# A decoder layer on one core: zero-padded score queries, cached memory in fours, the last FFN features padded, one group for the states' products

## The chip, the cores and the metric

The kernel runs on one core of a Trainium2 chip. The metric is the device time of one execution in microseconds (us); the median of three runs of the kernel before is 990.26 us (988.76 to 992.15).

## What is computed

One layer of a hybrid decoder, for 512 prompt rows and for 8 sampled sequences of 4 rows (32 sample rows) with the same weights, in 32-bit floats. Cut to what matters here:

```python
h = rms_norm(x, g_mix_pre); z = h @ w_in
# mLSTM heads (4 x 128): C is the state, one 128x128 matrix per sequence and head
num = w_inter * einsum('bhtd,bhde->bhte', qc, C) + ...      # product of queries and old state
C_new = decay * C + einsum('bhsd,bhse->bhde', wk, vc)
# differential attention (4 heads, two 64-dim components c, v = 128)
s = einsum('bqhcd,bkhcd->bhcqk', q, k) * DA_QK_DIM ** -0.5
p = softmax(where(mask, s, -inf)); a = p[:, :, 0] - lam * p[:, :, 1]
# prompt: 4 causal blocks of 128 queries; sample: 256 cached keys from pages
x = x + rms_norm(concat(h_ml, h_da) @ w_out, g_mix_post)
# cross attention (4 heads x 256) to 256 memory tokens; for the sample rows
# keys and values are cached: cache_mem_k, cache_mem_v (8, 256, 4, 256)
x = x + rms_norm(mem_attend(rms_norm(x, g_mem_pre), mk, mv) @ w_mo, g_mem_post)
# ConvFFN with 2752 = 21 * 128 + 64 features
u = h @ w_up; c = causal_conv3(u); f = (silu(g) * a) @ w_down
x = x + rms_norm(f, g_ffn_post)
```

## The kernel before

The program is one long list of work that a scheduler orders for each engine from the dependences, the buffers of the pools and its own estimates; the code's order is where it starts from. TensorE (PE) multiplies, VectorE (DVE) and ScalarE (ACT) evacuate and do the softmax arithmetic, GpSimd (POOL) helps, and SyncE's queue (SP) issues nearly all loads.

Weights go through `W`: a 512 KB load into a stage tile `wst` (pool `stg`, six of 128x1024), then `split` writes it as two f32r parts (ACT casts the high part, DVE subtracts for the low part) into a slot of pool `wp` (tag W, four slots `wslot`). A product is three f32r matmuls (L386 to L388 in `gemmA`, L1645 to L1647 for the FFN's second product). An f32 matmul that is not split takes two passes, so it shows as two rows in the trace.

A matmul can use part of the 128x128 array. The profile shows the tile as rows*columns behind the operation: `64*128` contracts over 64 rows, `128*32` gives 32 output partitions, as the sample's products do (32 rows for each of four heads, in four column tiles side by side).

The places that the change touches, in the order of time:

- `mls_update` (L954 to L959): for each head and each half of the eight sequences, the product of the queries `qzm` with the old states `csts` (`mlsi`), the new key-value product `mlus` (L957), and four state updates on VectorE (L959). The 32 `mlsi` products are made in two parts: 16 at the first step of the first half of the sequences, 16 at the first step of the second.
- `da_soft` (L1180, L1181): scores of one query block and head for the two components. Component 0 lies in partitions 0 to 63 of `dqT` and `dkT`, component 1 in 64 to 127; each score matmul takes its 64 rows, then a bf16 matmul adds the causal mask `cb`. Softmax follows on VectorE and ScalarE, the transposes `tpa` (L1196) and the product `oda` with the values (L1206). Block b has (b+1) * 128 keys, 16 block-head pairs in all. Between them the sample's cached keys are transposed (`tpk`, L1159) and scored (`ssc`, L1165), and the cached values are multiplied (`ops`, L1248).
- Cross attention: `mk_load`, `mk_turn` (16 half-sequences of cached keys, eight transposes `tpk` each, L1385) and `mk_scores` (8 matmuls `ssc` per sequence, L1395), one sequence after another with two turns between; `mv_load` (L1400) brings 1 MB of values per sequence into a W slot `vt`; `mv_out` (L1405) makes 8 matmuls `pso` per sequence. The prompt's own steps (scores `sca` L1336, transposes `cpt` L1354, values `cpo` L1366) are interleaved. The eight loads of `w_mo` share the stage tiles with the keys and the W slots with the values.
- FFN: 22 groups of features; the last one has 64 rows. `slotA` loads and splits the 64 rows of `w_down` by themselves, and the last products of L1645 to L1647 (and the sample's, L366) contract over 64 rows.

Of the kernel before, what the change touches and what calls it, by code (L numbers as in the profile page):

```python
# [7 lines left out]
F32 = mybir.dt.float32  # L8
# [7 lines left out]
P = 128  # L16
DM = 1024
SEQ = 512
NB = 8
# [54 lines left out]
def kernel(ctx: ExitStack, tc: tile.TileContext, I, O):  # L74
# [146 lines left out]
    def slotA(w, k0, n0, nrow=256, share=False):  # L221
        def emit():
            st, s = v2(stage(), 512), slot_tile()
            sv = s.rearrange("p l (k n) -> p l k n", k=2)
            r0 = k0 * P
            if nrow == 256:
                dma(out=st, in_=w[r0:r0 + 256, n0:n0 + 512].rearrange("(k p) n -> p k n", p=P))
                split_w(sv, st, share)
            else:
                for k, n in ((0, P), (1, nrow - P)):  # L230
                    dma(out=st[:n, k, :], in_=w[r0 + k * P:r0 + k * P + n, n0:n0 + 512])
                    split(sv[:n, 0, k, :], sv[:n, 1, k, :], st[:n, k, :])
            return sv, st
        W.add(emit)

# [712 lines left out]
    def mls_update(i):  # L948
        g, h = i // H, i % H
        cs_t = csts[g, h]  # L950
        if h == 0:
            for b in range(4):
                for k in range(H):
                    mm(pi[NS * k:NS * k + NS, 0:P], lhsT=qzm[:, 256 * k + (4 * g + b) * NS:256 * k + (4 * g + b + 1) * NS],  # L954
                       rhs=csts[g, k][:, b, :], start=(g + b == 0), stop=(g == 1 and b == 3))
        pu = at("mlus")
        mm(pu, lhsT=kS[:, h, :], rhs=vzs[i], start=True, stop=True)  # L957
        for b in range(4):
            STT(out=cs_t[:, b, :], in0=cs_t[:, b, :], scalar=dec[:, h, 4 + 4 * g + b:5 + 4 * g + b], in1=pu[:, b * P:(b + 1) * P],  # L959
                op0=MUL, op1=ADD)  # L960
        dma(out=O["s_ml_C"][0, 4 * g:4 * g + 4, h].rearrange("b d e -> d b e"), in_=cs_t)
        F.run(2.5)
# [207 lines left out]
    def da_soft(i):  # L1170
        b, h = i // H, i % H
        c0 = b * P
        nk = c0 + P
        pt = pts[i] = N("pda").rearrange("p (c k) -> p c k", c=2)
        nm = small(2, "nm")
        su = small(2, "su")
        sv = [mmp("sda")[:, :nk] for _ in range(2)]
        for c in range(2):
            rr = slice(64 * c, 64 * c + 64)
            mm(sv[c], lhsT=dqT[rr, h, c0:c0 + P], rhs=dkT[rr, h, 0:nk], start=True, stop=False)  # L1180
            mm(sv[c][:, c0:nk], lhsT=identb, rhs=cmaskb, start=False, stop=True)  # L1181
# [4 lines left out]
        nc.vector.reciprocal(out=rc, in_=su)  # L1186
# [191 lines left out]
    def mk_turn(i):  # L1378
        b, c = i // 2, i % 2
        if c == 0:  # L1380
            kts[b] = wp.tile([P, 8, 256], F32, name="kT", tag="W")
        for q in range(2):
            ps = at("tpk")
            for j in range(4):
                tr(ps[:, j * P:(j + 1) * P], kst[i][:, (4 * q + j) * P:(4 * q + j + 1) * P], ident)  # L1385
            (VCP if q else nc.scalar.copy)(out=kts[b][:, 4 * q:4 * q + 4, c * P:(c + 1) * P], in_=v2(ps, P))

    def mk_scores(i):
        b, c = i // 2, i % 2
        if c == 0:  # L1390
            return
        ps = mmp("ssc")[:, :256]
        for c in range(2):
            for h in range(H):
                mm(ps[NS * h:NS * h + NS], lhsT=qs[:, 2 * h + c], rhs=kts[b][:, 2 * h + c, :], start=(c == 0), stop=(c == 1))  # L1395
        sample_exp(sall, b, ps, nm, su)

    def mv_load(b):
        vts[b] = wp.tile([P, 2, DM], F32, name="vt", tag="W")
        dma(out=vts[b], in_=I["cache_mem_v"][0, b].rearrange("(c p) h d -> p c (h d)", p=P))  # L1400

    def mv_out(b):
        for c in range(2):
            for h in range(H):
                mm(pso[NS * h:NS * h + NS], lhsT=az[c][:, h, b * NS:(b + 1) * NS], rhs=vts[b][:, c, 256 * h:256 * h + 256],  # L1405
                   start=(b == 0 and c == 0), stop=(b == NB - 1 and c == 1))

    sall = S([P, NB, 256], F32, "cas")
    nm, su = small(NB, "snm"), small(NB, "ssu")
# [4 lines left out]
    for i, _ in enumerate(gemmB(hqT, [ev_q(m) for m in range(4, 8)])):  # L1414
        if i % 4 == 3:
            for j in (i // 2 - 1, i // 2):
                mk_turn(j)
                mk_load(j + 6)
    for b in range(NB):
        mk_scores(2 * b + 1)  # L1420
        if b < 4:
            for j in (2 * b + 8, 2 * b + 9):
                mk_turn(j)
                if j + 6 < 2 * NB:
                    mk_load(j + 6)
        else:
            mv_load(b - 4)
        if b % 2 == 1:
            next(prompt, None)
# [4 lines left out]
    for n0 in (0, 512):  # L1434
        slotsA(w_mo, n0)
    W.nslots = NSLOT
    for b in range(NB):
        if b >= 4:
            mv_load(b)
    W.pump()  # L1440
    for b in range(NB):
        mv_out(b)
        if b in VSTEPS:
            next(prompt, None)
    run(prompt)
    oS = Z("oS")[:, :256]
    nc.scalar.copy(out=oS, in_=pso)
# [106 lines left out]
    def gate(j, ua, ug, act, i):  # L1554
# [9 lines left out]
        VTT(out=a[:, :SEQ], in0=ca[:n, :SEQ], in1=cg[:n, :SEQ], op=MUL)  # L1564

        def sv(c):
            return c[:n, SEQ:].rearrange("p (b j) -> p b j", j=6)[:, :, 2:6]
        VTT(out=v2(a[:, SEQ:], TS), in0=sv(ca), in1=sv(cg), op=MUL)
        split(act[i // 2][:n, i % 2, 0, :], act[i // 2][:n, i % 2, 1, :], a)
        t = sm.tile([P, NS], F32, name="acs", tag="acs", bufs=5)  # L1570
        nc.gpsimd.tensor_copy(out=t[:n], in_=a[:, SEQ:])
        return t[:n]

    gf = gbc("g_ffn_post")
    acts, acss = {}, {}
# [44 lines left out]
    for gi, js in enumerate(groups):  # L1620
# [8 lines left out]
        behind = []  # L1629

        def one(b, ps, i, s):
            n = P if js[i] < 21 else 64
            t = act[i // 2][:n, i % 2]
            st, en = i == 0, i == nk - 1
            if b == 4:

# [5 lines left out]
                return  # L1642
            s = s[0]
            c0 = b * P
            mm(ps, lhsT=t[:, 0, c0:c0 + P], rhs=s[:n, 0, i % 2, :], start=st, stop=False)  # L1645
            mm(ps, lhsT=t[:, 0, c0:c0 + P], rhs=s[:n, 1, i % 2, :], start=False, stop=False)  # L1646
            mm(ps, lhsT=t[:, 1, c0:c0 + P], rhs=s[:n, 0, i % 2, :], start=False, stop=en)  # L1647

        def add_y(b, ps, n0):
            c = slice(n0, n0 + 512)  # L1650
# [152 lines left out]
```

## Time and profile before

| | before |
|---|---|
| median of 3 runs | 990.26 us |
| range | 988.76 to 992.15 us |
| profiled execution, its own time | 989.55 us |
| span in the profile | 987.8 us |
| mean granted TensorE clock | 0.993 |

How to read the rows: a group shows line, engine, operation, output<-inputs, shape and count, then busy time and the mean of one in ns, then idle time before it and what released it. A timeline row shows start, busy time, line and count; rows overlap because matmuls are pipelined, so the distance of two starts is the price of what lies between. An idle gap before a row is in square brackets with its releaser. The PE row of the page, in 40 slices, is at 9 tenths or more nearly everywhere:

```profile
PE   8999999999999999999999999999999999999994
DVE  6835325645786257633653569827757675685677
ACT  5754313334576357633543433342312222222232
POOL 6610000115231214400000354201100010110114
```

### The profile page before, as it was taken

How to read it: one execution, taken by the hardware profiler on the slowest of the kernel's cores; microseconds unless marked ns; L12 is line 12 of the kernel's file. 1: busy time of each engine (PE TensorE's matmuls, PEld its weight loads, DVE VectorE, ACT ScalarE, POOL GpSimd, SP SyncE). 2: the span in 40 equal slices, each digit the busy share in tenths (PEclk: the TensorE clock that was granted, in tenths of full speed). 3: DMA queues.
4: the chain of work that ended last, by engine and by line, in shares of the span. 5: the costliest groups of instructions: out<-in, count | busy, mean ns of one | idle time of the engine just before them, and what ended most of it. 6: DMA issues, size and time to landing. Idle time of an engine off the chain costs nothing.

```text
span 987.8 us, 17060 instructions
## 1 busy us (share of the span) xinstructions
PE 962.1 (97%) x6615; PEld 811.1 (82%) x6615; DVE 603.4 (61%) x1129; ACT 389.1 (39%) x746; POOL 195.5 (20%) x389
## 2 busy tenths in 40 slices
PE   8999999999999999999999999999999999999994
PEld 5899777789655878898767889989987997997983
DVE  6835325645786257633653569827757675685677
ACT  5754313334576357633543433342312222222232
POOL 6610000115231214400000354201100010110114
PEclk9999999999899999999999999999999999999998
DMA  8950222260835068765841764063053214304113
GB/s 283 301 161 1 86 75 91 63 206 12 255 109 177 21 219 266 261 219 168 304 171 49 233 197 127 6 171 86 4 139 103 74 42 117 118 26 141 31 47 112
DMA packets 120401, 130.26 MB, mean 132 GB/s; under 512 B 8423, under 2 KB 85832, under 8 KB 120320
## 3 DMA queue, kind: packets, MB, share of 16 engines
q1 hardware_dynamic: 114136, 125.69, 41.1%
q10 hardware_dynamic: 6184, 3.48, 1.2%
q8 instruction: 52, 0.85, 0.3%
q14 instruction: 29, 0.24, 0.1%
HBM read 112.22 MB, written 16.93 MB: 131 GB/s over the span
## 4 chain that ended last, share of the span: by engine, by line
PE 83%; DMA 6%; DVE 5%; issue 2%; ACT 2%; POOL 1%; SPq 1%; DVEq 0%; POOLq 0%; ACTq 0%
PE mm L455 30%; PE mm L386 5%; PE mm L387 5%; PE mm L388 5%; PE mm L443 5%; PE mm L1645 4%; PE mm L1647 4%; PE mm L1646 4%; PE mm L366 3%; PE sda L1180 2%; DMA xb<-x_d 2%; PE tpk L1385 2%; DMA xb<-in_x_prompt_dram 1%; DMA wst<-in_w_mk_dram 1%; PE cpo L1366 1%
## 5 line engine op out<-in xcount | busy, mean ns | idle before, releaser
L142 ACT CAST wslot<-wst 128x1024 fp32r<-128x1024 f32 (+1 forms) x127 | 131.0, 1036 | 273.3 <-issue 73.8
L455 PE MATMUL mm<-fT,wslot 128*128 128x256 f32 (+1 forms) x1872 | 235.7, 288 | 0.0
L455 PEld LDWEIGHTS mm<-fT,wslot 128*128 128x128 f32 x1872 | 234.7, 188 | 0.7 <-issue 0.4
L143 DVE TENSOR_TENSOR wslot<-wst,wslot 128x1024 fp32r<-128x1024 f32 (+1 forms) x127 | 154.9, 1222 | 91.8 <-ACT wslot L142 91.2
L1645 PE MATMUL mm<-wslot,act 128*128 128x512 f32 (+1 forms) x176 | 71.0, 405 | 0.0
L1646 PE MATMUL mm<-wslot,act 128*128 128x512 f32 (+1 forms) x176 | 69.5, 395 | 0.0
L1647 PE MATMUL mm<-wslot,act 128*128 128x512 f32 (+1 forms) x176 | 69.1, 397 | 0.0
L1546 POOL COPY cvo<-u 128x2 f32<-128x2 f32 x43 | 16.2, 377 | 221.3 <-DVE u L1544 221.3
L386 PE MATMUL mm<-wslot,hT 128*128 128x512 f32 x128 | 51.8, 407 | 0.0
L387 PE MATMUL mm<-wslot,hT 128*128 128x512 f32 x128 | 50.8, 397 | 0.0
L455 PE MATMUL mm<-hT,wslot 128*128 128x256 f32 (+1 forms) x384 | 50.7, 289 | 0.0
L388 PE MATMUL mm<-wslot,hT 128*128 128x512 f32 x128 | 50.6, 398 | 0.0
L455 PEld LDWEIGHTS mm<-hT,wslot 128*128 128x128 f32 x384 | 48.9, 188 | 0.5 <-issue 0.2
L1645 PEld LDWEIGHTS mm<-wslot,act 128*128 128x128 f32 (+1 forms) x176 | 33.4, 190 | 15.8 <-issue 7.8
L1541 DVE TENSOR_TENSOR u<-mm,rsb 128x256 f32<-128x256 f32 x43 | 18.1, 423 | 43.8 <-PE mm L455 43.8
L1647 PEld LDWEIGHTS mm<-wslot,act 128*128 128x128 f32 (+1 forms) x176 | 33.0, 188 | 7.7 <-issue 0.4
L1646 PEld LDWEIGHTS mm<-wslot,act 128*128 128x128 f32 (+1 forms) x176 | 33.1, 188 | 6.4
L1558 ACT ACTIVATE c<-c 128x560 f32<-128x560 f32 x21 | 14.1, 672 | 60.4 <-DVE c L1552 60.4
L1658 DVE TENSOR_TENSOR yp<-mm,yp 128x512 f32<-128x512 f32 x40 | 27.3, 688 | 13.7 <-PE mm L1647 13.6
L1552 DVE SCALAR_TENSOR_TENSOR c<-u,cvT,c 128x560 f32<-128x560 f32 x43 | 34.3, 797 | 0.8
L1551 DVE SCALAR_TENSOR_TENSOR c<-u,cvT,c 128x560 f32<-128x560 f32 x43 | 34.0, 792 | 0.1
L386 PEld LDWEIGHTS mm<-wslot,hT 128*128 128x128 f32 x128 | 24.1, 188 | 6.6 <-issue 2.1
(458 smaller groups left out, 1876.4 us busy)
## 6 DMA issues: line engine op xcount, KB each, us to landing
wst<-in_w_up_dram SPq DMA_DIRECT2D x42, 512.0 KB
wst<-in_w_in_dram SPq DMA_DIRECT2D x28, 512.0 KB
wst<-in_w_down_dram SPq DMA_DIRECT2D x20, 512.0 KB
wst<-in_cache_mem_k_dram SPq DMA_DIRECT2D x16, 512.0 KB
vt<-in_cache_mem_v_dram SPq DMA_DIRECT2D x8, 1024.0 KB
wst<-in_w_mk_dram SPq DMA_DIRECT2D x8, 512.0 KB
xb<-in_x_prompt_dram SPq DMA_DIRECT2D x8, 512.0 KB
wst<-in_cache_dk_dram SPq DMA_DIRECT2D x16, 256.0 KB
```

Source lines behind the costliest of these rows:

```text
L142: nc.scalar.copy(out=hi, in_=src)
L143: (eng or nc.vector).tensor_tensor(out=lo, in0=src, in1=f32(hi), op=SUB)
L386: mm(ps[b], lhsT=xt.hi(k, c0, c0 + n), rhs=s[:, 0, kk, :], start=(k == 0), stop=False)
L387: mm(ps[b], lhsT=xt.hi(k, c0, c0 + n), rhs=s[:, 1, kk, :], start=False, stop=False)
L388: mm(ps[b], lhsT=xt.lo(k, c0, c0 + n), rhs=s[:, 0, kk, :], start=False, stop=(k == nk - 1))
L443: mm(ps, lhsT=s[:, l, k, :], rhs=x(k, c0, c1), start=(k == 0 and j == 0), stop=(k == 7 and j == 2))
L455: mm(ps[i], lhsT=s[:, l, k, :], rhs=x(k, c0, c1), start=(k == 0 and j == 0), stop=(k == 7 and j == 2))
L1551: STT(out=c, in0=u[:, 1:EXT - 1], scalar=w[1], in1=c, op0=MUL, op1=ADD)
L1552: STT(out=c, in0=u[:, 0:EXT - 2], scalar=w[0], in1=c, op0=MUL, op1=ADD)
L1645: mm(ps, lhsT=t[:, 0, c0:c0 + P], rhs=s[:n, 0, i % 2, :], start=st, stop=False)
L1646: mm(ps, lhsT=t[:, 0, c0:c0 + P], rhs=s[:n, 1, i % 2, :], start=False, stop=False)
L1647: mm(ps, lhsT=t[:, 1, c0:c0 + P], rhs=s[:n, 0, i % 2, :], start=False, stop=en)
```

## The change

Four edits.

1. **Score queries.** A new tile `dqz` (128 x 4 x 512) gets component 1 of the prompt queries in partitions 64 to 127 (four ACT copies) and zeros in 0 to 63 (one POOL memset); partitions 64 to 127 of `dqT` are then zeroed for the prompt columns (four POOL memsets). A score of component 0 uses `dqT`, one of component 1 uses `dqz`, both over all 128 rows of `dkT`. The sum over the padded rows adds zeros.
2. **States' products.** `mls_update` makes all 32 `mlsi` matmuls at its first step.
3. **Cached memory.** Scores of sequences 0 to 3 are one stretch, then turns 8 to 15, then scores 4 to 7; `tc.issue_after` holds the turns and the second scores behind the named matmuls. Values are loaded in halves of 512 KB, sequences 0, 1, 2 and 7 into stage tiles, 3 to 6 into W slots, and are multiplied 0 to 3, then 4 to 7.
4. **Last features.** The stage rows and the activation `a` of the last 64 features are filled to 128 with zeros (POOL memsets), and split and multiplied like the others.

```diff
@@ slotA
+                nc.gpsimd.memset(st[nrow - P:, 1, :], 0.0)
                 for k, n in ((0, P), (1, nrow - P)):
                     dma(out=st[:n, k, :], in_=w[r0 + k * P:r0 + k * P + n, n0:n0 + 512])
-                    split(sv[:n, 0, k, :], sv[:n, 1, k, :], st[:n, k, :])
+                split(sv[:, 0], sv[:, 1], st)
@@ mls_update
-        if h == 0:
-            for b in range(4):
+        if i == 0:
+            for b in range(NB):
                 for k in range(H):
...
+                       rhs=csts[b // 4, k][:, b % 4, :], start=(b == 0), stop=(b == NB - 1))
@@ before dk_load
+    dqz = S([P, H, SEQ], F32, "dqz")
+    nc.gpsimd.memset(dqz[0:64], 0.0)
+    for b in range(4):
+        c = slice(b * P, b * P + P)
+        nc.scalar.copy(out=dqz[64:128, :, c], in_=dqT[64:128, :, c])
+        nc.gpsimd.memset(dqT[64:128, :, c], 0.0)
@@ da_soft
-            mm(sv[c], lhsT=dqT[rr, h, c0:c0 + P], rhs=dkT[rr, h, 0:nk], start=True, stop=False)
+            mm(sv[c], lhsT=(dqz if c else dqT)[:, h, c0:c0 + P], rhs=dkT[:, h, 0:nk], start=True, stop=False)
@@ mv_load
-        vts[b] = wp.tile([P, 2, DM], F32, name="vt", tag="W")
-        dma(out=vts[b], in_=I["cache_mem_v"][0, b].rearrange("(c p) h d -> p c (h d)", p=P))
+        if 2 < b < 7:
+            t = wp.tile([P, 2, DM], F32, name="vt", tag="W")
+            vts[b] = [t[:, 0], t[:, 1]]
+        else:
+            vts[b] = [stage(), stage()]
+        for c in range(2):
+            dma(out=vts[b][c], in_=I["cache_mem_v"][0, b, c * P:(c + 1) * P].rearrange("t h d -> t (h d)"))
@@ the loop over the cached memory
-    for b in range(NB):
-        mk_scores(2 * b + 1)
...
+    next(prompt)
+    for b in range(4):
+        t = mk_scores(b)
+    with tc.issue_after(t):
+        for j in range(8, 16):
+            t = mk_turn(j)
+            if j + 6 < 2 * NB:
+                mk_load(j + 6)
+            if j == 11:
+                next(prompt)
+    for b in range(3):
+        mv_load(b)
+    next(prompt)
+    with tc.issue_after(t):
+        for b in range(4, NB):
+            t = mk_scores(b)
+    for b in range(3, 7):
+        mv_load(b)
...
-    for b in range(NB):
-        if b >= 4:
-            mv_load(b)
+    for b in range(4):
+        mv_out(b)
+        if b == 0:
+            mv_load(7)
     W.pump()
-    for b in range(NB):
+    next(prompt, None)
+    next(prompt, None)
+    for b in range(4, NB):
         mv_out(b)
@@ the FFN's features, and its second product
-        a = T2([P, ROWS], "a")[:n]
+        a = T2([P, ROWS], "a")
+        if n < P:
+            nc.gpsimd.memset(a[n:], 0.0)
...
-            n = P if js[i] < 21 else 64
-            t = act[i // 2][:n, i % 2]
+            t = act[i // 2][:, i % 2]
...
-            mm(ps, lhsT=t[:, 0, c0:c0 + P], rhs=s[:n, 0, i % 2, :], start=st, stop=False)
+            mm(ps, lhsT=t[:, 0, c0:c0 + P], rhs=s[:, 0, i % 2, :], start=st, stop=False)
```

The order of the cached memory's transposes (`tpk`), scores (`ssc`) and the prompt's scores (`sca`, with the high part `qh` and the low part `ql` of the queries) on TensorE, before, from the first scores on:

```order
L1385 MATMUL tpk<-cpk,wst 128x128 x12
L1395 MATMUL ssc<-kT,qs 32x256 x14
L1385 MATMUL tpk<-cpk,wst 128x128 x4
L1395 MATMUL ssc<-kT,qs 32x256 x2
L1385 MATMUL tpk<-cpk,wst 128x128 x8
L1336 MATMUL sca<-mkT,qh 128x256 x2
```

and with the change, the same place, with the lines counted in the new file:

```order
L1344 MATMUL sca<-mkT,ql 128x256
L1401 MATMUL ssc<-kT,qs 32x256 x5
L1393 MATMUL tpk<-cpk,wst 128x128 x4
L1401 MATMUL ssc<-kT,qs 32x256 x27
L1393 MATMUL tpk<-cpk,wst 128x128 x12
```

and where the second four sequences are scored:

```order
L1344 MATMUL sca<-mkT,qh 128x256 x2
L1344 MATMUL sca<-mkT,ql 128x256
L1393 MATMUL tpk<-cpk,wst 128x128 x40
L1401 MATMUL ssc<-kT,qs 32x256 x32
L1362 MATMUL cpt<-cpk,cp 128x128 x4
```

The scores stood in twelve runs, of which the first two are shown, and stand in three.

SP's queue of loads in cross attention before: the last keys, `w_mo` in 512 KB pieces, the sample's rows `xb`, the values `vt` in 1 MB pieces, then the first `w_up`:

```order
L1376 DMA wst<-in_cache_mem_k_dram 128x1024
L227 DMA wst<-in_w_mo_dram 128x2x512 x2
L1095 DMA xb<-x_d_2554 32x1024
L227 DMA wst<-in_w_mo_dram 128x2x512 x2
L1400 DMA vt<-in_cache_mem_v_dram 128x2x1024 x2
L227 DMA wst<-in_w_mo_dram 128x2x512
L1400 DMA vt<-in_cache_mem_v_dram 128x2x1024
L227 DMA wst<-in_w_mo_dram 128x2x512
L1400 DMA vt<-in_cache_mem_v_dram 128x2x1024 x5
L227 DMA wst<-in_w_mo_dram 128x2x512 x2
L246 DMA wst<-in_w_up_dram 128x8x128 x6
```

and with the change:

```order
L1384 DMA wst<-in_cache_mem_k_dram 128x1024
L1096 DMA xb<-x_d_2554 32x1024
L1384 DMA wst<-in_cache_mem_k_dram 128x1024
L1413 DMA wst<-in_cache_mem_v_dram 128x1024 x6
L1413 DMA vt<-in_cache_mem_v_dram 128x1024 x8
L1413 DMA wst<-in_cache_mem_v_dram 128x1024 x2
L227 DMA wst<-in_w_mo_dram 128x2x512 x8
L247 DMA wst<-in_w_up_dram 128x8x128 x6
```

All eight `w_mo` loads, of which six stood ahead of the last five values, now stand behind all values.

TensorE where differential attention begins, before (the states' second products, then the scores of the first heads with their mask `cb`, in the code's own shapes):

```order
L954 MATMUL mlsi<-wst,qzm 32x128 x16
L957 MATMUL mlus<-vz,kS 128x512
L1180 MATMUL sda<-dkT,dqT 128x128
L1181 LDWEIGHTS cb
L1181 MATMUL sda<-cb 128x128
L1180 MATMUL sda<-dkT,dqT 128x128
```

and with the change:

```order
L958 MATMUL mlus<-vz,kS 128x512
L456 MATMUL mm<-hT_255,wslot 128x288
L1188 MATMUL sda<-dkT,dqT 128x128
L1189 LDWEIGHTS cb
L1189 MATMUL sda<-cb 128x128
L1188 MATMUL sda<-dkT,dqz 128x128
```

The second group of 16 `mlsi` products is gone from here (all 32 stand ahead of the first `mlus`), and every second score reads `dqz`.

More of the change, by code (lines that the diff above doesn't have):

```diff
@@ L1404, in mv_out @@
             for h in range(H):
-                mm(pso[NS * h:NS * h + NS], lhsT=az[c][:, h, b * NS:(b + 1) * NS], rhs=vts[b][:, c, 256 * h:256 * h + 256],
-                   start=(b == 0 and c == 0), stop=(b == NB - 1 and c == 1))
+                t = mm(pso[NS * h:NS * h + NS], lhsT=az[c][:, h, b * NS:(b + 1) * NS], rhs=vts[b][c][:, 256 * h:256 * h + 256],
+                       start=(b == 0 and c == 0), stop=(b == NB - 1 and c == 1))
+        return t.ins
     sall = S([P, NB, 256], F32, "cas")
@@ L1418 @@
                 mk_load(j + 6)
-    for b in range(NB):
-        mk_scores(2 * b + 1)
[L1421 to L1429, printed above, removed]
+    next(prompt)
[16 more added lines that the diff above has]
+        mv_load(b)
+    next(prompt)
     _, az = sample_softmax(sall, su, None, con("selX"), "ca")
```

31 lines of the change are left out of this document (13 added, 18 removed).

## The prediction

> **What bounds the kernel now.** I read the page from the top: engine totals, the chain that ended last, then the stages that the change touches.
>
> ```profile
> span 987.8 us, 17060 instructions
> PE 962.1 (97%) x6615; PEld 811.1 (82%) x6615; DVE 603.4 (61%) x1129; ACT 389.1 (39%) x746; POOL 195.5 (20%) x389
> PE 83%; DMA 6%; DVE 5%; issue 2%; ACT 2%; POOL 1%; SPq 1%; DVEq 0%; POOLq 0%; ACTq 0%
> ```
>
> TensorE is busy for 97% of the span and carries 83% of the chain; nothing else carries more than 6%. Time taken out of TensorE's stream therefore shortens the run, except where another engine already sets the pace. The stretches of the change, from the view of windows (length, then PE, PEld, DVE, ACT and POOL busy, then granted clock, DMA share, GB/s):
>
> ```profile
> 252.00:268.00 16.00, 13.94 (x86) 9.36 (x87) 12.20 (x46) 7.89 (x27) 1.71 (x5) 0.79 0.88 267
> 268.00:300.00 32.00, 30.74 (x213) 18.19 (x211) 25.46 (x70) 23.95 (x81) 13.70 (x15) 1.00 0.37 119
> 300.00:321.00 21.00, 21.00 (x209) 11.90 (x209) 14.85 (x26) 14.38 (x33) 2.02 (x3) 1.00 0.62 208
> 468.00:492.00 24.00, 24.00 (x210) 17.93 (x209) 15.37 (x37) 13.19 (x42) 0.00 (x0) 1.00 0.86 303
> 492.00:530.00 38.00, 38.00 (x274) 26.57 (x273) 20.83 (x46) 16.53 (x43) 0.00 (x0) 1.00 0.33 118
> 752.00:776.00 24.00, 24.00 (x130) 16.90 (x127) 15.28 (x24) 4.79 (x6) 1.28 (x9) 1.00 0.40 111
> ```
>
> Cross attention (468 to 530) and the FFN tail (752 to 776) have a TensorE that never stops: what goes there is gained in full. Differential attention (252 to 321) begins with idle TensorE, under half clock for part of it, and becomes saturated after 300.
>
> **The change part by part.** *Score queries over 128 rows.* The timeline of TensorE for one head late in that phase (start, busy, line, tile rows*columns; an f32 matmul shows as x2):
>
> ```profile
> 304.04 0.49 PE L1196 MATMUL tpa<-cpk,pda 128*128 128x128 f32 x3
> 304.46 1.12 PE L1180 MATMUL sda<-dkT,dqT 64*128 64x512 f32 x2
> 305.51 0.23 PE L1181 MATMUL sda<-cb 128*128 128x128 bf16 x1
> 305.67 1.12 PE L1180 MATMUL sda<-dkT,dqT 64*128 64x512 f32 x2
> ...
> 313.30 0.60 PE L1196 MATMUL tpa<-cpk,pda 128*128 128x128 f32 x4
> 313.83 1.12 PE L1180 MATMUL sda<-dkT,dqT 64*128 64x512 f32 x2
> ...
> 317.02 0.23 PE L1181 MATMUL sda<-cb 128*128 128x128 bf16 x1
> 317.09 1.11 PE L1206 MATMUL oda<-dvN,aT 128*128 128x128 f32 x8
> L1180 PE MATMUL sda<-dkT,dqT x64: 272/482/693, 251.9 to 320.3; 64*128 64x128 f32 x16, 64*128 64x256 f32 x16, 64*128 64x384 f32 x16, 64*128 64x512 f32 x16
> ```
>
> Rows of the timeline overlap, so I price by the distance of starts. Three passes of `tpa` take 0.42, four take 0.53: a pass of 128 columns and 128 rows costs 0.11 when nothing changes. A score plus its mask takes 305.67 − 304.46 = 1.21. Two passes of 512 columns at 0.11 per 128 are 0.88, and a mask followed by an instruction of the same tile shape takes 0.07 (317.02 to 317.09) where it takes 0.16 before the next 64-row score (305.51 to 305.67). The same work in one shape is then 0.93 to 0.95, a saving of 0.26 to 0.28; the surplus sits at the two changes of tile shape, 64*128 to 128*128 and back. The group has 64 passes, 32 scores, so at most 32 × 0.28 = 9.0 us.
>
> Not all of it arrives. The start of the phase:
>
> ```profile
> 255.83 0.47 PE L957 MATMUL mlus<-vz,kS 128*128 128x512 f32 x1 [1.07 <-DVE wst L959]
> 256.86 0.65 PE L967 MATMUL mlsn<-tb,mlD 32*32 32x128 f32 x8 [0.56 <-DVE rc L1186]
> ...
> 274.39 0.65 PE L1165 MATMUL ssc<-kT,qz 128*32 128x260 f32 x8 [0.67 <-DVE kT L1160]
> ```
>
> Until about 258 VectorE releases TensorE (its state updates, then the softmax), so the 8 scores of query block 0 (2.2 us) only enlarge these gaps: I count 0.3. Block 1 meets one more VectorE wait, 0.67 at 274: I count 1.5 of 2.2. Blocks 2 and 3, with TensorE nearly always busy, I count at 4.4 of 4.5. Sum **6.2**; the ends are 3 (VectorE and ScalarE at 25.5 and 24.0 of 32 us set the pace until 300, so that only block 3 and a little more count) and 9.0.
>
> The price of the second query tile: four copies 64x512 on ScalarE, one memset 64x2048 and four of 64x512 on POOL.
>
> ```profile
> L1160 ACT COPY kT<-tpk 128x512 f32<-128x512 f32 x8 | 4.7, 589 | 2.2 <-PE tpk L1159 2.0
> L1027 POOL MEMSET daz<- 128x2048 f32 x1 | 1.8, 1806 | 0.0
> ```
>
> By columns that is 4 × 0.59 = 2.4 on ScalarE and 1.8 + 4 × 0.45 = 3.6 on POOL, between 227 and 252. There TensorE runs projection matmuls that depend on neither, and the order puts the gate work that POOL delays by about 1.8 behind fourteen more of them. I take 0.2; without that cover the 1.8 would show.
>
> *The states' products in one group.* The row below is one of two such runs in the trace; the other begins at 241.03.
>
> ```profile
> 250.41 1.08 PE L954 MATMUL mlsi<-wst,qzm 128*32 128x128 f32 x32
> ```
>
> 32 passes on four column tiles are 8 after one another, 8 × 0.11 = 0.88 of the 1.08; the rest, 0.2, is entry and exit, of which there is one less, and the neighbour behind it is spared its own change of shape. The single group waits for all eight state tiles instead of four, with the first `mlus` and then projection matmuls queued behind it; both groups follow one another without an idle gap before them now, the later one inside 10 us: **0.3**, ends 0 and 0.4.
>
> *Cached memory in fours.*
>
> ```profile
> 457.15 1.93 PE L1395 MATMUL ssc<-kT,qs 128*32 128x256 f32 x28
> 459.01 0.66 PE L1385 MATMUL tpk<-cpk,wst 128*128 128x128 f32 x4
> 459.60 1.05 PE L1395 MATMUL ssc<-kT,qs 128*32 128x256 f32 x4
> 460.58 1.09 PE L1385 MATMUL tpk<-cpk,wst 128*128 128x128 f32 x8
> ...
> 482.89 1.06 PE L1395 MATMUL ssc<-kT,qs 128*32 128x256 f32 x12
> ...
> 501.55 0.50 PE L1366 MATMUL cpo<-pT,mvN 128*128 128x512 f32 x1
> 501.99 0.64 PE L1405 MATMUL pso<-vt,caz 128*32 128x256 f32 x8
> ```
>
> The matmuls of the four column tiles overlap, so a run costs as many steps as its fullest column has passes. x28 took 1.86 with 8 steps, x4 took 0.98 with 4 (its two matmuls share a column): 0.22 a step and 0.10 to 0.12 fixed. The four transposes between took 0.59 for 4 × 0.11: 0.15 more for being a detour. A broken run thus costs about 0.27. Before there are 12 runs (first 457.15, last 482.89) and 44 steps, as the uneven cuts leave columns empty; the new order has runs of 5, 27 and 32 matmuls, 34 steps. Saved: 10 × 0.22 + 9 × 0.27 = 4.6. The values fall from 9 runs and 36 steps to 6 runs and 38: a detour is dearer there (the lone `cpo` of 501.55 takes 0.44), 3 × 0.33 − 2 × 0.22 = 0.5. Together 5.1 at most.
>
> What could eat it is the queue of SP. Values and `w_mo` now stand as six, eight and two value loads and then eight `w_mo` loads:
>
> ```profile
> 484.09 24.23 SPq L1400 DMA_DIRECT2D vt<-in_cache_mem_v_dram  x5
> 512.88 0.50 PE L386 MATMUL mm<-wslot,oT 128*128 128x512 f32 x1
> ```
>
> Before, the last five values were issued from 484 as slots came free. Now six half-values go into stage tiles freed by the last transposes (about 468 to 474), eight into the slots of keys 4 to 7 (about 476), at up to 0.3 MB per us by the window's 303 GB/s: 7 MB need some 23 us, to about 495, while the first value product falls at about 492 and uses the earliest. The first four `w_mo` loads follow `mv_out(1)` and `(2)`, about 495, and 2 MB at that rate land by 502 against a first need near 508 (512.88 now, less what was saved). Behind the eight `w_mo` loads on SP stand only the first `w_up` loads, which are needed after this stage. I subtract 0.3 for waits: **4.8**; ends −1 (one stall of 6) and 5.1.
>
> *The last features padded.* Starts in the FFN tail:
>
> ```profile
> 753.04 0.40 PE L1645 MATMUL mm<-wslot,act 128*128 128x512 f32 x1
> 753.27 0.39 PE L1646 MATMUL mm<-wslot,act 128*128 128x512 f32 x1
> ...
> 755.42 0.50 PE L1645 MATMUL mm<-wslot,act 128*128 128x512 f32 x1
> ...
> 756.32 0.50 PE L1645 MATMUL mm<-wslot,act 64*128 64x512 f32 x1
> ```
>
> A pass costs 0.23, so three are 0.70; where 128 and 64 rows alternate, each triple takes 0.90 (755.42 to 756.32). The first pass of a triple shows 0.50 with 64 rows (756.32) as with 128 (755.42), so I take a pass to cost the same for either. The eight 64-row triples stand in seven runs, each with a change in and out: 7 × 2 × 0.2 = **2.8**, in full, since TensorE is busy 24.00 of 24. The padding costs three short memsets on a POOL that idles for 25.29 us up to 739.85; ends 2.4 and 3.1.
>
> ```profile
> 739.85 0.71 POOL L1546 COPY cvo<-u 128x2 f32<-128x2 f32 x1 [25.29 <-DVE u L1544]
> ```
>
> **Sum:** 6.2 − 0.2 + 0.3 + 4.8 + 2.8 = 13.9; less 0.5 for copies and order shifted elsewhere, 13.4. The profiled execution took 989.55 (span 987.8 and 1.75 around it), so it would take 976.2. The median of the three runs, 990.26, lies 0.7 above the profile; I take the middle, **976.5**.
>
> One rule of the skill speaks against the first part. The Trainium skill, "TensorE: Matmul & The Clock Gate", Part 3, says that matmuls of small contraction on different row groups run concurrently; by it two 64-row scores side by side would cost one, and padding would forfeit that, a loss of about 0.9 per pair. This trace does not show it: the two components start at 304.46 and 305.67, 1.21 apart, with the mask between them. So the sum stands without it.
>
> **The rivals.** *The attention phase is bound elsewhere.* Of 252 to 300, VectorE is busy 37.7 and ScalarE 31.8 of 48, and 3.3 us of TensorE are idle already. If the two softmax engines set that pace, scores give 3.0 and not 6.2: 979.7. Against it: TensorE is busy 30.74 of 32 between 268 and 300.
>
> *The clock.* The windows around the first gaps:
>
> ```profile
> 253.04:256.46 3.42, 2.19 (x10) 1.16 (x9) 2.93 (x13) 1.63 (x9) 0.00 (x0) 1.00 0.62 185
> 256.46:259.87 3.41, 2.58 (x17) 2.16 (x18) 2.56 (x12) 1.04 (x4) 0.00 (x0) 0.50 0.90 259
> ```
>
> A window with TensorE busy 2.19 of 3.42 is followed by 0.50 in the clock column; the 252 to 268 row averages 0.79. Shorter scores make that window emptier. If one further window of 3.4 runs at half clock, 1.7 us of work is lost, up to 3.4 with two: 978 to 980; if scores come earlier and the dip vanishes, up to 3.4 are gained: 973. The Trainium skill's page named above puts the throttle at an idle window; here no gap before it exceeded 1.07.
>
> *The change is not worth its loads (slower).* All eight `w_mo` loads now stand behind every value on one queue. Were the last value slot freed only with its product, as the five loads over 24.23 us from 484 show for before, the first `w_mo` tile would come after the values. TensorE needs it near 508; it decides from an arrival 13.4 us later, about 521. Before, the order kept six of eight ahead; if the four loads are issued at about 508 and need 7 us, with a 2.3 us split and the second half in the same state, I price 7 + 2.3 + 8 = 17: 993. Against it: values 0 to 2 and 7 no longer use those slots. Without the second half it is a partial stall, 5 to 9 us: 982 to 985.
>
> *It does not do what it says*, tile changes costing the same inside one shape: excluded for the FFN by 753.04 to 753.27, where equal shapes take 0.23.
>
> **How the numbers follow.** Forecast, 973.5 to 978.5: 0.57. Attention bound elsewhere or half clock longer, 978.5 to 981.5: 0.18. Partial stall on values or `w_mo`, 981.5 to 987: 0.09. Slower, 993: 0.04. All 17 us and the clock dip gone, 970 to 973.5: 0.12. The range 971.5 to 982.5 leaves out about 0.2 (a part of the top gain, the stalls, the slower case). About 0.3%, 3 us, is what a measurement of this kernel can tell from no change: faster 0.91, same 0.05, slower 0.04.
>
> **What would show it.** Scores with their mask at 0.93 and not 1.21 in 300 to 321 (first part); three `ssc` runs and six `pso` runs, with no idle TensorE before `pso` or the first `wslot,oT` (third); every FFN triple at 0.70 (fourth); a phase 252 to 321 shorter by 6. Wrong if TensorE's idle time in 252 to 300 grows by over 4, if an `oT` product waits for a `w_mo` split, or if half clock lasts longer than 6.8 us.

## The result, and the profile after

The changed kernel takes 977.06 us (975.15 to 981.35, four runs) beside 990.82 in the same runs of the kernel before: a ratio of 0.9869 with the 95% interval 0.9832 to 0.9906. Two later groups of runs of the same kernel gave 0.9834 (0.9811 to 0.9858) and 0.9865 (0.9849 to 0.9880). The gain is 1.3 to 1.7%; the prediction of 976.5 is 0.6 us off the first median. The profiled execution took 977.42 us with a span of 975.6.

The page of the changed kernel, the span, the engine totals and the chain that ended last:

```profile
span 975.6 us, 17090 instructions
PE 948.0 (97%) x6615; PEld 815.0 (84%) x6615; DVE 599.8 (61%) x1127; ACT 389.6 (40%) x748; POOL 200.2 (21%) x397
PE 85%; DMA 5%; DVE 5%; ACT 2%; issue 1%; POOL 1%; SPq 0%; DVEq 0%; POOLq 0%; ACTq 0%
```

TensorE has as many instructions as before and is busy for 14.1 us less. Where the 12.1 us between the two profiled executions lie is read from the timeline of TensorE, by the start of the same instruction in both:

| instruction on TensorE | before | after | difference | of it in this stretch |
|---|---|---|---|---|
| first sample product of the projection | 102.19 | 102.77 | +0.58 | +0.58 |
| first prompt score `sda` | 251.86 | 251.38 | −0.48 | −1.06 |
| first product with `mixT` | 320.94 | 314.61 | −6.33 | −5.85 |
| last projection product of the memory queries | 455.62 | 449.11 | −6.51 | −0.18 |
| last product with `w_mo` | 567.97 | 557.36 | −10.61 | −4.10 |
| first FFN product | 570.45 | 561.08 | −9.37 | +1.24 |
| first conv transpose `cvo` | 624.40 | 615.91 | −8.50 | +0.87 |
| last FFN product | 974.57 | 962.43 | −12.14 | −3.64 |

The four stretches in which the change works are 1.06 + 5.85 + 4.10 + 3.64 = 14.65 us shorter in this profile, and the rest of the program is 2.5 longer. Two more profiles of the same changed kernel (after_again and after_third_time) give 14.89 and 14.40 for the four stretches, but 4.0 longer and 1.8 shorter for the rest, so the rest varies between executions and is not a cost that belongs to the change. The pieces in turn, first the scores, timeline of after:

```profile
298.48 1.02 PE L1188 MATMUL sda<-dkT,dqT 128*128 128x512 f32 x2
299.34 0.22 PE L1189 MATMUL sda<-cb 128*128 128x128 bf16 x1
299.39 1.08 PE L1188 MATMUL sda<-dkT,dqz 128*128 128x512 f32 x2
300.31 0.22 PE L1189 MATMUL sda<-cb 128*128 128x128 bf16 x1
300.46 1.08 PE L1256 MATMUL ops<-wst,daz 128*32 128x128 f32 x32
```

A score of 512 columns with its mask took 1.21; the first here takes 0.91 (298.48 to 299.39). The second takes 1.07, since its mask is followed by the column tiles of `ops`: 0.15 from 300.31 to 300.46, where the first mask hands over in 0.05.

The cached memory's scores, timeline of after:

```profile
452.06 1.05 PE L1401 MATMUL ssc<-kT,qs 128*32 128x256 f32 x10
453.04 0.65 PE L1393 MATMUL tpk<-cpk,wst 128*128 128x128 f32 x4
453.62 3.22 PE L1401 MATMUL ssc<-kT,qs 128*32 128x256 f32 x54
...
467.69 3.66 PE L1401 MATMUL ssc<-kT,qs 128*32 128x256 f32 x64
471.28 0.66 PE L1362 MATMUL cpt<-cpk,cp 128*128 128x128 f32 x4
```

Three runs instead of twelve: 0.98 + 3.16 + 3.59 = 7.7 us, where the twelve of before take 11.0 by the same measure, with no idle TensorE before any product that waits for a value or a `w_mo` load. The products with the values (`pso`) fall from nine runs to six, but these take 8.95 us for 8.96: nothing is gained there. And one wait is new. TensorE stands idle before the transposes `ost` of the finished sample rows, which it did not before:

```profile
502.14 0.44 PE L1474 MATMUL ost<-cpk,oS 128*128 128x128 f32 x2 [0.69 <-ACT oS L1471]
```

In the two other profiles of this kernel the same wait is 0.86 and 1.41 us.

The FFN tail, first before, then after:

```profile
751.13 1.18 PE L366 MATMUL mm<-wst,acs 128*32 128x256 f32 x8
752.24 0.50 PE L1645 MATMUL mm<-wslot,act 128*128 128x512 f32 x1
```

```profile
742.64 0.64 PE L367 MATMUL mm<-wst,acs 128*32 128x256 f32 x8
743.21 0.50 PE L1670 MATMUL mm<-wslot,act 128*128 128x512 f32 x1
743.54 0.39 PE L1671 MATMUL mm<-wslot,act 128*128 128x512 f32 x1
743.77 0.39 PE L1672 MATMUL mm<-wslot,act 128*128 128x512 f32 x1
744.00 0.40 PE L1670 MATMUL mm<-wslot,act 128*128 128x512 f32 x1
```

Besides the triples, now 0.70 each in steady state, each of the sample's two groups fell from 1.11 to 0.57. The timeline merges its shapes; the view of the line keeps them apart, first before, then after:

```profile
L366 PE MATMUL mm<-wst,acs x8: 376/390/403, 751.1 to 751.9; 128*32 128x256 f32 x4, 64*32 64x256 f32 x4
L367 PE MATMUL mm<-wst,acs x8: 379/391/404, 742.6 to 742.9; 128*32 128x256 f32 x8
```

Before, the four 128-row passes start in two pairs (751.13 and 751.37) and the four 64-row passes in two more (751.68 and 751.92). After, all eight have one shape and start in two fours (742.64 and 742.88), on four column tiles at once. So the group goes from four steps to two; the change of shape itself adds only 0.07 (0.31 from 751.37 to 751.68 for 0.24).

The 2.5 us of this profile lie between. In front of the FFN:

```profile
557.36 0.40 PE L389 MATMUL mm<-wslot,oT 128*128 128x512 f32 x1
557.69 0.40 PE L1538 MATMUL rsb<-cpk,rsd 32*128 32x32 f32 x2
560.43 0.80 PE L1538 MATMUL rsb<-cpk,rsd 128*128 128x128 f32 x2 [2.34 <-DVE ht L320]
```

TensorE idles 2.34 us for the norm (1.10 before), and half clock (a granted TensorE clock of 0.50) follows from 560.35 for 6.83 us. There is half clock from 96.13 for 3.41 us too, in a stretch that the change does not touch, and from 256.56 for 6.83, where the kernel before has it as well.

### The profile page after: what moved, and what is told of

Read it like the earlier page. It is cut to its first block, busy times and chain, and to the rows that moved or that the text cites. A ratio compares the mean times of both kernels' runs of the same rounds, so it can differ in the third digit from the quotient of the medians.

```text
span 975.6 us, 17090 instructions
## 1 busy us (share of the span) xinstructions
PE 948.0 (97%) x6615; PEld 815.0 (84%) x6615; DVE 599.8 (61%) x1127; ACT 389.6 (40%) x748; POOL 200.2 (21%) x397
## 4 chain that ended last, share of the span: by engine, by line
PE 85%; DMA 5%; DVE 5%; ACT 2%; issue 1%; POOL 1%; SPq 0%; DVEq 0%; POOLq 0%; ACTq 0%
PE mm L456 31%; PE mm L444 8%; PE mm L387 6%; PE mm L389 6%; PE mm L388 6%; PE mm L1670 4%; PE mm L1672 4%; PE mm L1671 4%; PE mm L367 3%; PE sda L1188 2%; DMA wst<-in_w_mo_dram 1%; PE oda L1214 1%; DMA xb<-x_d 1%; PE tpk L1393 1%; PE tpk L1168 1%
## 5 line engine op out<-in xcount | busy, mean ns | idle before, releaser
L142 ACT CAST wslot<-wst 128x1024 fp32r<-128x1024 f32 x125 | 130.8, 1050 | 271.7 <-issue 82.0
L143 DVE TENSOR_TENSOR wslot<-wst,wslot 128x1024 fp32r<-128x1024 f32 x125 | 154.7, 1239 | 94.1 <-ACT wslot L142 94.0
L1670 PE MATMUL mm<-wslot,act 128*128 128x512 f32 x176 | 69.8, 398 | 0.0
L1671 PE MATMUL mm<-wslot,act 128*128 128x512 f32 x176 | 69.6, 396 | 0.0
L1672 PE MATMUL mm<-wslot,act 128*128 128x512 f32 x176 | 69.1, 397 | 0.0
L1670 PEld LDWEIGHTS mm<-wslot,act 128*128 128x128 f32 x176 | 33.5, 190 | 11.9 <-issue 4.5
L1672 PEld LDWEIGHTS mm<-wslot,act 128*128 128x128 f32 x176 | 33.1, 188 | 7.7 <-issue 0.4
L1671 PEld LDWEIGHTS mm<-wslot,act 128*128 128x128 f32 x176 | 33.1, 188 | 6.9
L1582 ACT ACTIVATE c<-c 128x560 f32<-128x560 f32 x21 | 14.1, 672 | 59.8 <-DVE c L1576 59.8
```

Of the source, the lines that this page charges most:

```text
L142: nc.scalar.copy(out=hi, in_=src)
L143: (eng or nc.vector).tensor_tensor(out=lo, in0=src, in1=f32(hi), op=SUB)
L1670: mm(ps, lhsT=t[:, 0, c0:c0 + P], rhs=s[:, 0, i % 2, :], start=st, stop=False)
L1671: mm(ps, lhsT=t[:, 0, c0:c0 + P], rhs=s[:, 1, i % 2, :], start=False, stop=False)
L1672: mm(ps, lhsT=t[:, 1, c0:c0 + P], rhs=s[:, 0, i % 2, :], start=False, stop=en)
```

## The experiments

Every edit is to the changed kernel unless it says otherwise. "The phase" is the time from the start of the first prompt score to that of the last mask.

**Scores back to 64 rows (e1).**

```diff
-    dqz = S([P, H, SEQ], F32, "dqz")
...
-            mm(sv[c], lhsT=(dqz if c else dqT)[:, h, c0:c0 + P], rhs=dkT[:, h, 0:nk], start=True, stop=False)
+            mm(sv[c], lhsT=dqT[rr, h, c0:c0 + P], rhs=dkT[rr, h, 0:nk], start=True, stop=False)
```

> The kernel after with the score queries as before (64-row tiles, no second query tile); the other three parts stay. From the first score to the last mask the profile of before shows 68.98 us (251.86 to 320.84) and that of after 63.04. Theory (the gain of that phase is the change of tile shape at each score): 68 to 70, scores of 512 columns with their mask 1.21 again, total about 5.5 to 6 above after, near 983. Rival (the gain of that phase comes from the states' products and the altered order around it): the phase stays at 63 to 65 and the total within 2 of 977.

Measured: phase 68.48, total 982.85 (980.71 to 983.91), ratio 0.9923 (0.9899 to 0.9946). The timeline of TensorE:

```profile
306.28 1.12 PE L1182 MATMUL sda<-dkT,dqT 64*128 64x512 f32 x2
307.33 0.23 PE L1183 MATMUL sda<-cb 128*128 128x128 bf16 x1
307.49 1.12 PE L1182 MATMUL sda<-dkT,dqT 64*128 64x512 f32 x2
```

1.21 again: the theory. The phase is 5.4 us longer than in after (5.8 and 5.9 against its two other profiles) and the total 5.8. The phase alone undercounts the padding a little: one product `mlus` stands ahead of the first score in e1 (253.87 to 254.18, 0.31 us) and behind it in after. From the first sample product to the first product with `mixT`, where TensorE has the same products in both, e1 takes 217.91 and after 211.84, 211.46 and 211.40: the padding is worth 6.1 to 6.5.

**The two 64-row scores side by side (e2).** Query tiles as in e1.

```diff
         for c in range(2):
             rr = slice(64 * c, 64 * c + 64)
-            mm(sv[c], lhsT=dqT[rr, h, c0:c0 + P], rhs=dkT[rr, h, 0:nk], start=True, stop=False)
-            mm(sv[c][:, c0:nk], lhsT=identb, rhs=cmaskb, start=False, stop=True)
+            t = mm(sv[c], lhsT=dqT[rr, h, c0:c0 + P], rhs=dkT[rr, h, 0:nk], start=True, stop=False)
+        with tc.issue_after(t.ins):
+            for c in range(2):
+                mm(sv[c][:, c0:nk], lhsT=identb, rhs=cmaskb, start=False, stop=True)
```

> As e1_scores_64, but the two 64-row scores of a head are issued next to each other and both masks follow. Theory (only the changes of tile shape cost): most heads have one 64-row stretch in place of two, so about 16 x 0.28 = 4.5 us less than e1, the phase at 64 to 66; the two scores of 512 columns still follow one another, about 0.9 to 1.05 apart. Rival (the Trainium skill's rule on small contractions in different row groups, under which padding forfeits something): the two scores overlap, starting 0.1 to 0.3 apart, a pair of 512 columns takes about 1.1 in place of 2.1, and the phase falls to 57 to 61, below after.

Measured: phase 66.23, total 978.94 (976.22 to 982.35), ratio 0.9896 (0.9862 to 0.9930). The timeline of TensorE:

```profile
298.53 1.13 PE L1182 MATMUL sda<-dkT,dqT 64*128 64x512 f32 x4
299.59 0.28 PE L1185 MATMUL sda<-cb 128*128 128x128 bf16 x2
299.81 1.08 PE L1252 MATMUL ops<-wst,daz 128*32 128x128 f32 x32
...
313.85 1.12 PE L1200 MATMUL tpa<-cpk,pda 128*128 128x128 f32 x4 [1.75 <-DVE pda L1192]
```

All four passes, two scores of 512 columns, end by 299.59: 1.06 for what takes 2 × 1.05 one after the other. The pair with both masks takes 1.28, against 1.98 padded (298.48 to 300.46). So the rival was right on TensorE: the two 64-row tiles of different rows overlap here when nothing stands between them, and did not with a mask between them. The Trainium skill, "TensorE: Matmul & The Clock Gate", Part 3, says that small matmuls on different tiles of the array run concurrently; this trace agrees, with 1.06 for the pair. The rival's phase of 57 to 61 did not come, though: TensorE waits more, here 1.75 for the softmax.

**Only query block 0 padded (e3).**

```diff
+            rr = slice(64 * c, 64 * c + 64) if b else slice(0, P)
+            mm(sv[c], lhsT=(dqT if b or not c else dqz)[rr, h, c0:c0 + P], rhs=dkT[rr, h, 0:nk], start=True, stop=False)
```

> The kernel after with only query block 0 padded (8 of 32 scores, 128 columns each); blocks 1 to 3 in 64-row tiles. Theory (VectorE sets the pace up to about 258, so these eight are worth next to nothing): the phase from first score to last mask is within 0.8 of e1_scores_64. Rival (every padded score counts 0.28): 2.2 shorter than e1.

Measured: phase 67.53, 0.95 below e1, one profile (total 982.88, one run). That is just outside the bound of the theory and less than half of the rival's 2.2. Of the 0.95, 0.30 comes before the first sixteen key transposes and the rest behind them.

**Cached memory as before (e4).** Loads, scores and values of the kernel before:

```diff
-    for b in range(4):
-        t = mk_scores(b)
-    with tc.issue_after(t):
-        for j in range(8, 16):
...
+    for b in range(NB):
+        mk_scores(2 * b + 1)
```

> The kernel after with the cached memory's loads, scores and values as before; the other three parts stay. From the last projection product of the memory queries to the last product with w_mo the profile of before shows 112.35 us (455.62 to 567.97) and that of after 108.25 (449.11 to 557.36). Theory: 112 to 112.7 here, and the idle gap of TensorE in front of the FFN is near 1.1 again (2.34 in after) with no half clock behind it, so that of the 4.1 some 3 are given back and the total is only 0.5 to 2 above after. Rival (the gap and the half clock in front of the FFN have nothing to do with this part): the gap stays above 2 or the half clock is there, and the total is 4 above after, near 981.

Measured: 112.15 for the stretch; total 978.99 (977.57 to 979.80), ratio 0.9889 (0.9868 to 0.9911). Against the three profiles of after (108.25, 108.40 and 108.94) that makes this part worth 3.9, 3.8 and 3.2. The three differ by the wait before `ost`: less 0.69, 0.86 and 1.41 they are 107.56, 107.54 and 107.53, and e4 has no such wait. So the part gains 4.6 and gives 0.7 to 1.4 of it back there. In front of the FFN:

```profile
561.00 0.40 PE L389 MATMUL mm<-wslot,oT 128*128 128x512 f32 x1
561.33 0.40 PE L1522 MATMUL rsb<-cpk,rsd 32*128 32x32 f32 x2
562.43 0.49 PE L1522 MATMUL rsb<-cpk,rsd 128*128 128x128 f32 x2 [0.70 <-DVE ht L320]
```

The gap is small and no half clock follows, as expected, and the total is 1.9 above after (2.3 and 3.5 above its two later groups). But e1, e2 and e3, which have the new memory part, show gaps of 0.89, 0.63 and 0.61 there. The 2.34 is therefore not shown to come from this part.

**The changed kernel again, as a control.** No edit.

> The kernel after once more, unchanged, as a control for the places of half clock. Its profile above has half clock at 96.13 (3.41 us), 256.56 (6.83) and 560.35 (6.83) and an idle gap of 2.34 us in front of the FFN. Theory (the 256 stretch belongs to the program, the one at 96 and the one in front of the FFN hang on how the windows of 3.41 us fall): 256 there again, the other two shorter or missing in at least one place; total 975 to 979. Rival (all three belong to the changed program): all three at the same places with the same lengths.

Measured: 976.69 (974.03 to 978.66). Half clock from 257.75 for 6.83 us; from 97.32 for 3.41; in front of the FFN only 3.41, behind a gap of 0.84; and from 8.57 and 397.69, 3.41 each. The third profile (after_third_time) has it from 255.09 for 6.83 and from 558.88 for 3.41, with a gap of 0.87. The theory: only the stretch at 256 comes each time with its full length, and the gap of 2.34 was one execution's. What varied in that execution is not settled.

**FFN tail in 64 rows (e5).** The padding of `a`, of the stage rows and of the products taken back.

```diff
-            t = act[i // 2][:, i % 2]
+            n = P if js[i] < 21 else 64
+            t = act[i // 2][:n, i % 2]
```

> The kernel after with the last FFN features in 64 rows as before. The stretch from the first conv output transpose to the last FFN product takes 350.17 us in the profile of before and 346.53 in after, e1, e2 and e3. Theory: 350.1 to 350.3 here, of it about 1.1 at the two groups of sample products (1.11 each for 0.57) and 2.5 at the triples. Rival (part of the 3.6 is the clock or another part of the change): below 349.5.

Measured: 350.17 for the stretch, to the hundredth that of before, and 346.52 or 346.53 in every other profile with this part. All 3.64 belongs to it.

**Idle TensorE filled (f1).** The products of zeros are added; their results are not used.

```diff
+        if i > 3:
+            with tc.issue_after(t.ins):
+                for _ in range(3):
+                    mm(pi[:, P:], lhsT=warm[:, 0:P], rhs=warm[:, P:], start=True, stop=True)
...
+    fl = at("fill")
+    with tc.issue_after(last[0].ins):
+        for _ in range(8):
+            mm(fl, lhsT=warm[:, 0:P], rhs=warm, start=True, stop=True)
```

> The kernel after with idle TensorE filled: three bf16 products of zeros (384 columns) behind each of the last four state products, two behind the mlsn group, and eight of 512 columns behind the last product with w_mo; their results are not read. Theory (half clock follows a window in which TensorE does little): no half clock at 256 to 263 and none in front of the FFN; 263 is reached about 3 us earlier than in after, total 972 to 975. Rival (the throttle does not look at that, or the pace there is VectorE's): half clock stays or its loss is only replaced by VectorE's pace, total 976 to 979.

Measured: 976.17 (974.45 to 978.96). The profile has no half clock between 13 us and the tail, and from the first score to the first `mlt` transpose takes 11.66 instead of 13.79 us. But the total is that of after. Timed longer, beside the unchanged kernel:

> f1_fill_gaps once more, timed longer. Its profiled execution had no half clock inside the program and was 3 us shorter than that of after, but its median of four was 976.17 beside 976.69. Theory (the fillers keep the clock up in most executions): median 1.5 to 3 below after_third_time. Rival (the other variation between executions hides it, or the fillers' gain is VectorE's to give): within 1.

> The kernel after unchanged, timed beside f1_again. Median 976 to 978; half clock at 256 to 264 for 6.8 us in the profile again.

Measured: 975.84 (973.36 to 977.48) and 975.54 (973.38 to 976.38). The theory fell: the totals are equal. Two views of windows over three parts of the phase (first score to first `mlt`, to 296, to the first product with `mixT`), first f1_again, then the unchanged kernel, show where the gain goes in this pair:

```profile
249.86:261.52 11.66, 10.57 (x87) 6.69 (x85) 10.65 (x42) 7.55 (x24) 1.82 (x5) 1.00 0.66 198
261.52:296.00 34.48, 33.10 (x292) 22.94 (x289) 30.59 (x84) 26.79 (x93) 14.13 (x17) 1.00 0.56 186
296.00:312.55 16.55, 15.33 (x149) 9.03 (x147) 11.39 (x18) 11.57 (x26) 1.77 (x3) 1.00 0.75 247
```

```profile
249.64:263.50 13.86, 11.06 (x73) 7.85 (x71) 10.66 (x42) 7.52 (x24) 1.86 (x5) 0.75 0.72 217
263.50:296.00 32.50, 31.64 (x287) 22.31 (x284) 28.21 (x84) 26.87 (x94) 13.91 (x16) 1.00 0.52 175
296.00:312.43 16.43, 15.82 (x153) 9.59 (x153) 11.78 (x19) 11.81 (x27) 2.01 (x3) 1.00 0.74 251
```

With the full clock (1.00 for 0.75) the first part is 2.2 us shorter and the second 2.0 longer, VectorE busy 30.59 of 34.48 in it. From the first score to the first product with `mixT` it is 62.69 and 62.79. The first profile, f1_fill_gaps, has 61.79, against 62.79 to 63.23 in the three of the unchanged kernel, so there 1.0 to 1.4 arrived. In front of the FFN the eight fillers add 1.2 (3.50 and 3.49 from the last product with `w_mo` to the first of the FFN, for 2.22 and 2.25 in the last two profiles of the unchanged kernel), a gap of 0.7 stays behind them, and half clock (from 562.21) came in f1_again all the same. So the equal totals also hold what the second set of fillers cost; the fillers of the phase were not timed alone.

**Adjacent scores with fillers (f2).** Both edits, e2 and f1.

> e2_scores_adjacent with the same fillers as f1_fill_gaps. e2 showed two adjacent 64-row scores of 512 columns in about 1.06 together, but gaps of 1.3 and 1.75 that end on the softmax engines, and half clock at 255.66 and 313.69. Theory (with scores this cheap the softmax engines set the pace of the phase): phase 62 to 65, no better than padding, total 973 to 977. Rival (e2's phase was long only for its half clock): phase 58 to 61, total 969 to 972.

Measured: phase 66.12, total 981.64 (978.78 to 985.23). The profile has no half clock between 14 us and the tail, and the phase is as long as in e2: half clock was not its reason. It is longer than the theory had it, too.

**Without the row maximum (g1, g2).** Both leave out the maximum that the softmax subtracts.

```diff
-            VRED(out=nm[:, c:c + 1], in_=sv[c], axis=AX.X, op=MAX, negate=True)
-            ACT(out=pt[:, c, :nk], in_=sv[c], func=AF.Exp, bias=nm[:, c:c + 1], accum_out=su[:, c:c + 1])
+            ACT(out=pt[:, c, :nk], in_=sv[c], func=AF.Exp, bias=zb, accum_out=su[:, c:c + 1])
```

> The kernel after without the row maximum in the prompt's differential-attention softmax (the 32 reductions of VectorE go, the exponential takes a bias of 0). Theory (after about 268 the softmax engines share the pace with TensorE): the stretch from the first mlt transpose to the first product with mixT, 49.45 us in after, falls to 45 to 48. Rival (TensorE alone sets the pace there once scores are padded): 48.8 to 49.5.

Measured: 52.01, outside both (total 982.04, one run). The new order puts a `soT` activation between two exponentials, so that ScalarE loads its table twice more, as its timeline shows:

```profile
252.81 1.28 ACT L989 ACT_TABLE_LOAD   x1
254.11 0.66 ACT L989 ACTIVATE soT<-soT 128x544 f32<-128x544 f32 x1
254.78 1.28 ACT L1193 ACT_TABLE_LOAD   x1
```

TensorE then idles 4.32 us before 257.92, and half clock lasts 10.24, from 255.69. Both lie ahead of the stretch that was to be measured (it begins at 267.70); inside it TensorE idles 1.93 us for `kT` before 276.02, and half clock comes again from 276.17 for 3.41, which costs 1.7 at most. Even without that, 50.3 is no shorter than the 49.45 of after, although VectorE is relieved of 32 reductions. The order on ScalarE changed as well, so the experiment neither shows nor rules out that VectorE sets the pace of the padded kernel.

> e2_scores_adjacent without the row maximum, as g1_after_no_max. The stretch from the first mlt transpose to the first product with mixT is 54.80 us in e2, though its adjacent 64-row scores overlap. Theory (e2 is long because its masks, and so the softmax, wait for both scores, and VectorE and ScalarE set the pace): with the reductions gone 46 to 50, a larger gain than in g1. Rival (e2 is long because scores with another shape between them cost TensorE more): still 53 or more.

Measured: 48.07 against 54.80 in e2, phase 61.02; one run at 974.31. The view of windows from the first `mlt` to 296, g2:

```profile
264.10:296.00 31.90, 31.29 (x277) 19.68 (x277) 21.06 (x63) 25.70 (x90) 13.45 (x16) 1.00 0.42 143
```

With VectorE's load down to 21.06 of 31.90 TensorE is busy 98% of it. The theory, in one profile: e2 was long because the softmax could not follow. Leaving out the maximum also shortens the way from a score to its exponential, and how much that, VectorE's load and the later masks each have to do with it was not tried apart.

No version tried that keeps the row maximum beats the changed kernel: f1 is equal within the spread.

## Why the prediction was right

**Scores.** The step "32 × 0.28 = 9.0 at most, 6.2 realised" was right in mechanism and in size: e1 measures 6.1 to 6.5 over the two stretches with equal work, and 5.8 in the total. How it divides over the blocks was less right: block 0 gave 0.95 where 0.3 was counted (e3, one profile). Only four of its eight scores stand ahead of VectorE's waits, and there the gain is 0.30, as counted; the other four begin at 262.98 to 267.21 in before, behind those waits.

**Copies and memsets of the second tile.** Counted at −0.2 and hidden, as they are: from the first sample product to the first score after takes 148.61 us in all three profiles and e1, without them, 149.33. Of the 0.7, 0.31 is the product `mlus` that after makes behind the first score; the rest comes with the new order there, which no run took apart.

**States' products.** Counted 0.3; before to e1, the same stretch goes from 149.67 to 149.33; with the phase it goes from 218.75 to 217.91, so 0.8 may be its worth. One profile of before tells no more than that.

**Cached memory.** 4.8 was counted, 3.2 to 3.9 measured (e4). The run prices held: 4.6 was counted for the scores, and the part gains 4.6 before its wait. The 0.5 for the values did not come (`pso` 8.95 for 8.96): their detours were priced from one lone `cpo`. The 0.3 taken off for waits stood for the loads, which came in time, so the slower rival did not happen; the wait that came, 0.7 to 1.4 for `oS` before `ost`, was not in the sum.

**FFN.** The mechanism was right and the term too small: 2.8 counted, 3.64 measured (e5). The step left out the two sample groups, 2 × (1.11 − 0.57) = 1.1, which gain by four column tiles working at once and not by the change of shape that the step priced; the triples give the other 2.5.

**Together.** The four stretches gave 14.4 to 14.9 in the three profiles against 13.9 summed: scores and states' products 6.9 to 7.4 for 6.3, the FFN 3.6 for 2.8, and the cached memory less than its 4.8. The 0.5 kept back for the rest stood against 2.5, 4.0 and −1.8 there. In the first profile that is 1.2 at the norm, 0.6 ahead of the first sample product and 0.9 in the stretch with half clock at 560; in the others the same places have other lengths, and there is one profile of the kernel before to compare with. By the medians of three groups of runs the gain is 13.8, 15.2 and 13.8, where 13.4 was forecast. So the forecast is right by its mechanism; that it comes within 0.6 us, when its terms miss by 0.6 to 1.6 in both directions, is luck.

**Rivals.** "Attention bound elsewhere" (3.0 for the scores) did not come to pass in the kernel as changed, but e2, f1 and f2 suggest that its edge is near: of the 2 us that f1 takes out of the start of the phase, 0.1 to 1.4 arrive at its end, and e2's overlap of 0.7 per pair does not shorten its phase below that of after. That VectorE alone is the edge is not shown (g1). "The clock" stayed at 6.83 us around 256, though over the whole program ahead of the tail half clock lasts 17.07, 20.47 and 10.24 us in the three profiles of after and 6.83 in the one of before. The prediction's sentence that the trace does not show concurrent row tiles was true of that trace; that nothing is forfeited was not: e2 shows 0.7 per pair of 512 columns that padding gives up, without a way here to collect it.

## What to carry to other kernels

Where TensorE is the bound, count its changes of tile shape: here a score lost 0.3 us to its two changes and an FFN triple 0.20 to each, and padding with zeros or grouping equal shapes took them out. Look at tiny groups as well: padding let the sample's products use four column tiles at once. Before padding a small contraction, try its two row tiles next to each other; here they overlapped with nothing between them and not with a mask between them. And price a gain in a phase whose other engines are at 85% by what they will let through: here 2.2 us of clock regained at the start became 0.1 to 1.4 at the end of the phase.

## What the runs showed of the hardware that was not expected

- Two f32 matmuls in `64*128` tiles on different rows, 512 columns, two passes each, took 1.06 us together (e2), 1.05 each when a mask stood between (before).
- Ahead of the tail, half clock came in pieces of 3.41 us: 3.41, 6.83 or 10.24 in every profile here. In most cases TensorE was idle, in pieces, for 0.4 us (e1, before 258.03) to 2.8 us (g1, before 255.69) of the 3.41 us in front of it. But in four profiles (two of after, e3, e4) it also came at 96 to 97 us, behind a stretch of tiny matmuls (4x4 and 4x8) in which the profile has TensorE busy 6.00 of 6.00 us; before and the third profile of after show the same stretch without it. What decides it is not shown.
- Fillers took half clock away at 256 in all three profiles that had them, and in front of the FFN in two of three. At 256 that gained 2.0 to 2.2 us there, and 0.1 to 1.4 at the end of the phase.
